# Hybrid encoder layer: one split copy of x without its norm, mean squares taken by token, rope tables built first, queries rotated by halves on VectorE

## The chip, the cores and the metric

The kernel runs on one core of a Trainium2 chip. The metric is the device time of one execution in microseconds (us). Before the change, three runs gave 942.72, 944.30 and 948.27 us, median 944.3 us.

## The reference, cut to what matters

One layer of an encoder over 512 tokens with 1024 features, in float32:

```python
h = rmsnorm(x, g_mix)                      # x * rsqrt(mean(x*x) + EPS) * g_mix
proj = h @ w_in                            # 1024 x 5376
aq, ak, av, hq, hf_f, hf_b, hi, hg, gate_a, gate_b = split(proj)
attn_o = bidir_gqa(aq, ak, av, q_norm, k_norm)     # RMSNorm per head, axial rotary, 8 q heads, 2 kv heads
hgrn_o = hgrn2_bidir(hq, hf_f, hf_b, hi, hg, ...)  # gated recurrence, 4 heads, two directions, chunks of 32
merged = sigmoid(gate_a) * (attn_o @ w_attn_branch) + sigmoid(gate_b) * (hgrn_o @ w_hgrn_branch)
x = x + merged @ w_out
x = x + hier_moe(rmsnorm(x, g_ffn), ...)   # 32 experts, top 2 of one group of 8
```

The norm of a token is one number per row of `h`. So `rmsnorm(x, g) @ w` equals `((x * g) @ w)` with each row multiplied by that number afterwards; the change turns on this. The rotary step takes neighbouring pairs (a, b) of a head to (a cos - b sin, a sin + b cos).

## The kernel before, in words

**Precision.** A float32 product is made of three TensorE passes: each operand is split into a high part and the rest (`h_`, `l_`), and `mm3` (lines 257 to 260) adds high x high, high x low and low x high into the same PSUM bank. Activations are split once, weights when they arrive: `wsplit` (lines 241 to 255) takes a loaded weight tile `wr` of 128x1024, has ScalarE copy it to `wh` (line 250) and VectorE subtract (line 251, `wl`). There are two `wh` and two `wl` buffers, so a split cannot start before TensorE is done with the split two before it.

**Projections.** `w_in` is cut into chunks. Seven "token" chunks of 256 columns (`proj_tok`, 96 matmuls of 128x256 each, two weight tiles of 48 matmuls) put tokens on the partitions: chunk 0 holds keys and values, 1 and 2 the queries, 3 and 4 the values of the recurrence, 5 and 6 its output gates. Twenty-eight "feature" chunks of 128 columns (`proj_fm`, 24 matmuls of 128x512, one weight tile) put features on the partitions: for each of the four recurrence heads two forget gates and a query, then 16 branch gates.

**The start.** SP issues all loads, in the order in which the code is written; there are three `wr` buffers. x arrives transposed in eight pieces `xr` of 128x512. For each, lines 184 and 185 make a first split set `yh`, `yl` of x times `g_mix` without the norm (tile name `m`); ScalarE squares the piece and GpSimd adds the squares up (lines 190 and 191). Chunk 0 runs on this first set, piece by piece as it comes. `norm_x` (lines 204 to 217) sums the squares over partitions with a matmul by ones (line 207), works out the inverse root as a 128x512 tile `rbc`, and transposes it to get `rst`, one number per token (line 216). Chunks 1 and 2 also run on the first set; their norm comes in later through `rst`. Meanwhile `norm_parts` (lines 219 to 228) makes a second split set `xh`, `xl` (tile name `x`) with the norm in it: per piece one VectorE multiply (line 224), one ScalarE copy (225) and one GpSimd subtraction (226). All later projections, but chunk 3, run on the second set.

**Queries and keys.** After chunk 3 the pool of the x pieces is closed, a new pool is opened in its memory, and the rope tables are loaded and multiplied by the q and k norms (lines 332 to 343, tiles `cg` and `sg`). Lines 351 to 375 take the mean squares per head and rotate: ScalarE makes a copy `sw` with the pair elements swapped (368), GpSimd multiplies it by the sine table (372), VectorE multiplies by the cosine table (373), adds (374) and scales by the norms (375), for k in four 128x128 steps and for all eight q heads in four 128x512 steps.

**The heads.** For each recurrence head h: attention scores of two q heads (`att_scores`: scores in PSUM, a maximum over four tiles on VectorE, line 423, then over partitions with GpSimd's `partition_all_reduce`, line 424, a subtraction on VectorE, 426, and an exponential on ScalarE, 427), the recurrence in both directions (`hgrn_dir`), one token chunk, the attention output (`att_out`, lines 435 and 441), and the recurrence's output. GpSimd also does small steps of `hgrn_dir` (lines 524, 540, 545 to 547, 561) and scales the output gates (481). Each forget gate, query and branch gate leaves PSUM by one VectorE `tensor_scalar` with a lower bound (lines 519, 631 and 600).

**The rest.** The branches are multiplied by their gates, `w_out` is applied, the router picks experts, and the weights of all 32 experts stream in (line 781) through a ring of buffers; the first ring buffers become free when the projections are done.

**The order of the work.** SP's queue and the expert matmuls follow the code. On the other queues a list scheduler sorts the instructions by its own cost model; each queue then runs strictly in that order.

## Time and profile before

| | |
|---|---|
| median of 3 runs | 944.3 us |
| the profiled execution | 945.72 us, its span 944.0 us |
| mean granted TensorE clock | 0.988 |
| TensorE busy | 880.5 us (93%) |
| VectorE busy | 439.1 us (47%) |
| ScalarE, GpSimd busy | 267.4 us, 125.8 us |
| read from HBM | 245.11 MB, 264 GB/s over the span |

PE is TensorE's matmuls, PEld its weight loads, DVE VectorE, ACT ScalarE, POOL GpSimd, SP SyncE. In a timeline row the first number is the start, the second the time that the merged instructions cover, both in us; then the engine, the line, the operation, out<-in by tile names, the shape and the count, and in brackets the idle time ahead and what ended it. In a table by windows each engine has its busy us and its count; PEclk is the granted clock. Matmuls overlap, so their own durations (0.39 us for 128x512) are longer than the distance from one start to the next.

### The profile page before, as it was taken

What the parts mean: (1) busy time and instruction counts of PE and PEld (TensorE: products, weight loads), DVE (VectorE), ACT (ScalarE), POOL (GpSimd) and SP (SyncE); (2) the same over time, 40 slices, a digit from 0 to 9 for tenths busy, and PEclk for the clock granted to TensorE, in tenths of its full rate; (3) what the DMA queues carried; (4) which work ended last, traced back from release to release, by engine and by line L of the source; (5) the groups of instructions that cost most, each with busy time, mean ns of one, the idle gap of its engine ahead of it and who ended that gap; (6) DMA issues with size and microseconds to landing.
All of it is one profiled execution on the core that took longest, in us unless ns stands there. A gap on an engine that the chain in (4) does not pass through costs nothing. (4 is left out here: it accounts for less than half of the span.)

```text
span 944.0 us, 12699 instructions
## 1 busy us (share of the span) xinstructions
PE 880.5 (93%) x5098; PEld 556.5 (59%) x5099; DVE 439.1 (47%) x805; ACT 267.4 (28%) x461; POOL 125.8 (13%) x136
## 2 busy tenths in 40 slices
PE   6899989998999999999899999999979889799896
PEld 5798758784867888889744433444424344243433
DVE  6999857876864445433524222423213132031233
ACT  5556646665662545431100000000000000000000
POOL 4543322223310011100111000000000000000000
PEclk9999999998999999999999999999999999999998
DMA  6222201111111222896789999999999999999993
GB/s 225 70 99 90 68 23 68 46 53 60 45 68 62 95 90 89 315 416 249 291 335 348 408 420 417 419 418 420 417 420 420 417 420 419 419 419 419 420 405 133
DMA packets 49646, 246.25 MB, mean 261 GB/s; under 512 B 7024, under 2 KB 12912, under 8 KB 25776
## 3 DMA queue, kind: packets, MB, share of 16 engines
q1 hardware_dynamic: 44304, 238.32, 63.3%
q0 software_dynamic: 2160, 3.94, 1.2%
q10 hardware_dynamic: 3120, 3.15, 1.0%
q8 instruction: 42, 0.69, 0.3%
q14 instruction: 20, 0.16, 0.1%
HBM read 245.11 MB, written 4.19 MB: 264 GB/s over the span
## 5 line engine op out<-in xcount | busy, mean ns | idle before, releaser
L1062 PE MATMUL b<-e,wr 128*64 128x512 f32 x720 | 177.0, 597 | 9.4 <-DMA e<-in_wu 8.7
L1062 PEld LDWEIGHTS b<-e,wr 128*64 128x64 f32 x720 | 56.7, 136 | 104.2 <-issue 82.5
L1069 ACT ACTIVATE gt<-b,sw 128x512 f32<-128x512 f32 x16 | 11.0, 687 | 320.4 <-PE b L1062 320.4
L1090 DVE TENSOR_TENSOR t<-b,t 128x512 fp32r<-128x512 f32 (+1 forms) x33 | 22.2, 673 | 148.5 <-ACT t L1089 148.5
L1087 PE MATMUL b<-e,gt 128*64 128x512 f32 (+1 forms) x368 | 81.7, 575 | 9.6 <-DMA e<-in_wd 8.8
L260 PE MATMUL b<-x,wl 128*128 128x512 f32 x224 | 88.3, 394 | 1.0 <-DVE wl L251 1.0
L258 PE MATMUL b<-x,wh 128*128 128x512 f32 x224 | 88.1, 393 | 0.8 <-ACT hv L330 0.8
L259 PE MATMUL b<-x,wh 128*128 128x512 f32 x224 | 88.0, 393 | 0.0
L250 ACT ACTIVATE wh<-wr 128x1024 fp32r<-128x1024 f32 (+1 forms) x60 | 61.4, 1025 | 80.0 <-PE b L259 47.3
L251 DVE TENSOR_TENSOR wl<-wr,wh 128x1024 fp32r<-128x1024 f32 (+1 forms) x60 | 78.1, 1302 | 11.3 <-ACT wh L250 11.1
L1062 PE MATMUL b<-x,wr 128*64 128x512 f32 x264 | 64.0, 597 | 2.7 <-DMA x<-in_wu 2.7
L1087 PEld LDWEIGHTS b<-e,gt 128*64 128x64 f32 x368 | 26.5, 137 | 60.9 <-issue 45.2
L258 PE MATMUL b<-wh,m 128*128 128x256 f32 x176 | 51.1, 294 | 10.7 <-ACT wh L250 6.5
L1070 DVE SCALAR_TENSOR_TENSOR gt<-b,sw,gt 128x512 f32<-128x512 f32 x16 | 12.0, 750 | 104.1 <-PE b L1062 94.4
L1022 POOL DMA_INDIRECT xs<-xd,ix x15 | 15.3, 1019 | 290.1 <-DVE sw L1025 155.7
L1089 ACT ACTIVATE t<-b 128x512 fp32r<-128x512 f32 (+1 forms) x33 | 19.3, 584 | 122.1 <-PE b L1087 122.1
L259 PE MATMUL b<-wl,m 128*128 128x256 f32 x176 | 51.9, 295 | 1.8 <-DVE wl L251 1.7
L260 PE MATMUL b<-wh,m 128*128 128x256 f32 x176 | 51.1, 292 | 1.3 <-DVE m L185 1.3
L1106 PE MATMUL b<-t,wl 128*128 128x512 f32 (+1 forms) x132 | 51.4, 392 | 0.0
L1107 PE MATMUL b<-t,wl 128*128 128x512 f32 (+1 forms) x132 | 50.5, 385 | 0.4 <-DVE t L1090 0.4
L260 PEld LDWEIGHTS b<-x,wl 128*128 128x128 f32 x224 | 42.1, 188 | 10.7 <-DVE wl L251 1.5
L258 PEld LDWEIGHTS b<-x,wh 128*128 128x128 f32 x224 | 42.1, 188 | 10.2 <-ACT hv L330 1.0
(328 smaller groups left out, 1594.9 us busy)
## 6 DMA issues: line engine op xcount, KB each, us to landing
e<-in_wg SPq DMA_DIRECT2D x45, 1024.0 KB, 19.9
e<-in_wu SPq DMA_DIRECT2D x45, 1024.0 KB, 20.4
e<-in_wd SPq DMA_DIRECT2D x42, 1024.0 KB, 19.9
x<-in_wd SPq DMA_DIRECT2D x19, 1024.0 KB, 19.9
x<-in_wg SPq DMA_DIRECT2D x17, 1024.0 KB, 17.7
x<-in_wu SPq DMA_DIRECT2D x16, 1024.0 KB, 19.9
wr<-in_wfm SPq DMA_DIRECT2D x28, 512.0 KB, 3.5
wr<-in_wtok SPq DMA_DIRECT2D x12, 512.0 KB, 3.4
```

The lines of the kernel that those rows point to most:

```text
L250: SA.activation(h_[:, ks], r[:, ks], AF.Copy)
L251: V.tensor_tensor(l_[:, ks], r[:, ks], f(h_)[:, ks], op=ALU.subtract)
L258: PE.matmul(o, ah, bh, start=first, stop=False)
L259: PE.matmul(o, ah, bl, start=False, stop=False)
L260: PE.matmul(o, al, bh, start=False, stop=last)
L1022: G.indirect_dma_start(xs[q, b], None, xd[:, :], bass.IndirectOffsetOnAxis(ap=ix[:, b], axis=0), bounds_check=S - 1, oob_is_err=False)
L1062: PE.matmul(o[j * 64:(j + 1) * 64, :], hT[half][:, k, b * P + j * 64:b * P + (j + 1) * 64], ring[(n, e, half)](k), start=(half == 0 and k ...
L1087: PE.matmul(o[j * 64:(j + 1) * 64, 0:w], hidT[:, k * P + j * 64:k * P + (j + 1) * 64], ring[("wd", e, n)](k)[:, c:c + w], start=(k == 0), ...
L1089: SA.activation(y[:, 2 * n, c:c + w], o[:, 0:w], AF.Copy)
L1090: V.tensor_tensor(y[:, 2 * n + 1, c:c + w], o[:, 0:w], f(y)[:, 2 * n, c:c + w], op=ALU.subtract)
L1106: PE.matmul(p_[:, 0:w], l, y[:, 2 * n, c:c + w], start=(i == 0), stop=False)
L1107: PE.matmul(p_[:, 0:w], l, y[:, 2 * n + 1, c:c + w], start=False, stop=(i == len(ys) - 1))
```

## The change

- x is split once, without the norm, into tiles `x` (`yh`, `yl`); `norm_parts` and the second set are gone. Every later projection runs on this one set, and the norm is multiplied in when a result leaves PSUM: by token in token chunks (`scale=rst`, or a `tensor_scalar` per token tile), and in feature chunks by `normed`, a `tensor_tensor` with `rbc` from PSUM and then a `tensor_scalar` for the lower bound.
- The mean squares no longer come from the transposed pieces. x is loaded a second time by token, four tiles `xt` of 128x1024 (2 MB), and ScalarE squares each with a running sum. `rst` comes from that directly; `rbc` is built from it by four VectorE broadcasts and four TensorE transposes (`norm_wide`). The matmul by ones and GpSimd's sums are gone.
- The x pieces have four buffers in place of eight; the `at` tiles three in place of four. The loads of w chunk 1, the rope tables, `xt` and the identity stand right behind the x pieces in SP's queue.
- The rope tables have a pool of their own and are built first. `rotate` runs once for k and once for each half of q, behind the chunk that yields it; the swapped product is two VectorE instructions on every second element, and ScalarE's swapped copy and GpSimd's product are gone.

```diff
+    big = [tl(U, [P, 4, 512], "x", F32R, bufs=4) for _ in range(4)]
     for k in range(NK):
-        r = tl(RA, [P, 512], "xr", bufs=8)
+        r = tl(RA, [P, 512], "xr", bufs=4)
         SY.dma_start(r, A["xT"][:, k, :])
...
-        h_, l_ = mt(F32R), mt(F32R)
+        h_, l_ = big[k // 4][:, k % 4], big[2 + k // 4][:, k % 4]
         SA.activation(h_, r, AF.Copy, scale=gmix[:, k:k + 1])
         V.scalar_tensor_tensor(l_, r, gmix[:, k:k + 1], f(h_), op0=ALU.mult, op1=ALU.subtract)
-        if k == 0:
-            SA.activation(sqs, r, AF.Square)
-        else:
-            sq = tl(RA, [P, 512], "sq", bufs=2)
-            SA.activation(sq, r, AF.Square)
-            G.tensor_tensor(sqs, sqs, sq, op=ALU.add)
...
+    w1 = [tl(U, [P, 4, 256], "wr", bufs=3)]
+    SY.dma_start(w1[0], A["wtok"][1, :, 0:4])
+    qkn = cload("qkn", [P, 2, 64], pool=C1)
+    rope = cload("rope", [P, 2, NT, 64], pool=RB)
+    xts = []
+    for t in range(NT):
+        xts.append(tl(RA, [P, D], "xt", bufs=4))
+        SY.dma_start(xts[t], A["xtok"][:, t, :])
+    ident = cload("ident", [P, P])
...
+            SA.activation(tl(RA, [P, D], "sq"), xts[t], AF.Square, accum_out=ms[:, t:t + 1])
...
+            wide = tl(RA, [P, P], "wide", bufs=4)
+            V.tensor_copy(wide, rst[:, t:t + 1].to_broadcast([P, P]))
+            PE.transpose(p_[:, t * P:(t + 1) * P], wide, ident)
...
-            V.scalar_tensor_tensor(xr[k], xr[k], gmix[:, k:k + 1], rbc, op0=ALU.mult, op1=ALU.mult)
-            SA.activation(h_, xr[k], AF.Copy)
-            G.tensor_tensor(l_, xr[k], f(h_), op=ALU.subtract)
...
+    def normed(z, p_):
+
+        V.tensor_tensor(z, p_, rbc, op=ALU.mult)
+        V.tensor_scalar(z, z, -ZMAX, None, op0=ALU.max)
...
-            SA.activation(sw.rearrange("p (c b) -> p c b", b=2), src.rearrange("p (c b) -> p c b", b=2)[:, :, ::-1], AF.Copy)
...
-            G.tensor_tensor(t2.rearrange("p (h d) -> p h d", d=64), sw.rearrange("p (h d) -> p h d", d=64), sb, op=ALU.mult)
+            for i in range(2):
+                V.tensor_tensor(t2.rearrange("p (h c b) -> p h c b", c=32, b=2)[:, :, :, i],
+                                o.rearrange("p (h c b) -> p h c b", c=32, b=2)[:, :, :, 1 - i],
+                                sg[:, w, t, :].rearrange("p (c b) -> p c b", b=2)[:, :, i].unsqueeze(1)
+                                .to_broadcast([P, nh, 32]), op=ALU.mult)
             V.tensor_tensor(ov, ov, cb, op=ALU.mult)
             V.tensor_tensor(o, o, t2, op=ALU.add)
             V.tensor_tensor(ov, ov, b3(qn[:, t, a:b], nh, 64), op=ALU.mult)
...
-            V.tensor_scalar(o, res[j], -ZMAX, None, op0=ALU.max)
+            for t in range(2):
+                V.tensor_scalar(o[:, t], res[j][:, t], rst[:, 2 * j + t:2 * j + t + 1], -ZMAX, op0=ALU.mult, op1=ALU.max)
...
-        V.tensor_scalar(z, p_, -ZMAX, None, op0=ALU.max)
+        normed(z, p_)
```

The scheduler's order moves too. First VectorE's queue where the weights of chunks 1 and 2 are split. Before, from the fifth of the eight products by `rbc` (L224, `xr` are the pieces of x) to the second half of chunk 2 (`wl_445` and `wl_449` are its halves):

```order
L224 SCALAR_TENSOR_TENSOR xr_122<-xr_122,c_gmix_80,rbc_291 128x512
L224 SCALAR_TENSOR_TENSOR xr_133<-xr_133,c_gmix_80,rbc_291 128x512
L224 SCALAR_TENSOR_TENSOR xr_142<-xr_142,c_gmix_80,rbc_291 128x512
L224 SCALAR_TENSOR_TENSOR xr_152<-xr_152,c_gmix_80,rbc_291 128x512
L251 TENSOR_TENSOR wl_445<-wr_440,wh_444 128x1024
L216 COPY rst_304<-hg_299 128x4
L347 TENSOR_TENSOR rs_99_712<-rst_304 128x4
L251 TENSOR_TENSOR wl_449<-wr_442,wh_448 128x1024
```

And after, between the first and the second half of chunk 1, at whose second half (`wl_364`) it ends (`t_60` holds squares of k, `t_61` and `t_62` swapped products of k, `c_lb` the lower bounds):

```order
L212 TENSOR_SCALAR ms_280<-ms_280 128x4
L343 TENSOR_REDUCE qs_321<-t_60_324 128x4x2
L358 TENSOR_TENSOR qk_314<-qk_314,cg_270 128x128
L315 TENSOR_TENSOR lmx_301<-c_lb_260 128x8
L358 TENSOR_TENSOR qk_314<-qk_314,cg_270 128x128
L359 TENSOR_TENSOR qk_314<-qk_314,t_61_335 128x128
L317 TENSOR_TENSOR c_lb_260<-c_lb_260,lmx_301 128x8 x2
L203 TENSOR_TENSOR rst_49_291<-rst_290 128x4
L359 TENSOR_TENSOR qk_314<-qk_314,t_62_341 128x128
L248 TENSOR_TENSOR wl_364<-wr_256,wh_363 128x1024
```

The products by `rbc` that stood ahead of a weight split are gone. Ahead of `wl_364` now stand steps of the rotation of k, among them a row that needs all four sums of squares (L212) and one that needs a constant loaded late (L315).

Second, GpSimd's queue in the second recurrence head. A row that reads only ISA stands wherever the queue goes from ordinary instructions to the all-reduce or back; the ISA row with tile names is the all-reduce itself. Before (`at_1389` and `at_1542` are the maxima of q heads 2 and 3):

```order
L547 TENSOR_TENSOR log_134_836<-log_134_836 128x4x2
L561 TENSOR_TENSOR qt_1628<-e_277_1575,fac_1617 128x512
L424 ISA
L424 ISA at_1389<-at_1388 128x512
L424 ISA at_1542<-at_1541 128x512
L524 ISA
L524 TENSOR_TENSOR k_1967<-k_1967,sg_1969 128x512
```

And after (`at_1369` and `at_1524` are the same two maxima):

```order
L549 TENSOR_TENSOR log_117_811<-log_117_811 128x4x2
L425 ISA
L425 ISA at_1369<-at_1368 128x512
L563 ISA
L563 TENSOR_TENSOR qt_1611<-e_260_1557,fac_1600 128x512
L425 ISA
L425 ISA at_1524<-at_1523 128x512
L526 ISA
L526 TENSOR_TENSOR k_1953<-k_1953,sg_1955 128x512
```

The two all-reduces stood side by side; now the product `qt` stands between them, with an ISA row on each side.

Third, the same queue in the third recurrence head. Before (`at_1899` is the maximum of q head 4):

```order
L540 COPY end_137_839<-z_2081 128x4x4
L545 TENSOR_TENSOR log_133_835<-log_133_835 128x4x4
L546 TENSOR_TENSOR log_133_835<-log_133_835 128x4x2
L547 TENSOR_TENSOR log_133_835<-log_133_835 128x4x2
L424 ISA
L424 ISA at_1899<-at_1898 128x512
L561 ISA
L561 TENSOR_TENSOR qt_2138<-e_361_2085,fac_2127 128x512
```

And after (`at_1884` is the same maximum):

```order
L542 COPY end_120_814<-z_2068 128x4x4
L425 ISA
L425 ISA at_1884<-at_1883 128x512
L547 ISA
L547 TENSOR_TENSOR log_116_810<-log_116_810 128x4x4
L548 TENSOR_TENSOR log_116_810<-log_116_810 128x4x2
L549 TENSOR_TENSOR log_116_810<-log_116_810 128x4x2
L563 TENSOR_TENSOR qt_2126<-e_344_2072,fac_2115 128x512
```

Here the number of ISA rows is the same, but the three small sums of the backward direction now stand behind the all-reduce.

## The prediction

> **What bounds the kernel now.** I read the page first, for the span and the DMA rate by slices, then busy time by windows, then who waited for whom, then timelines around the waits.

> ```profile
> span 944.0 us, 12699 instructions
> ...
> GB/s 225 70 99 90 68 23 68 46 53 60 45 68 62 95 90 89 315 416 249 291 335 348 408 420 417 419 418 420 417 420 420 417 420 419 419 419 419 420 405 133
> ```

> ```profile
> 24.00:66.00 42.00, 37.44 (x298) 36.76 (x296) 38.09 (x64) 21.97 (x43) 22.58 (x15) 0.96 0.27 95
> 138.00:184.00 46.00, 46.00 (x375) 35.30 (x373) 38.03 (x69) 28.68 (x50) 10.56 (x15) 1.00 0.17 58
> 184.00:238.00 54.00, 50.26 (x382) 37.14 (x381) 38.56 (x68) 31.94 (x55) 15.96 (x18) 0.94 0.15 50
> 480.00:944.00 464.00, 430.77 (x2032) 185.20 (x2028) 128.85 (x256) 30.28 (x49) 16.78 (x17) 0.99 0.97 398
> ```

> ```profile
> 388.08 2.02 SPq L781 DMA_DIRECT2D e<-in_wg  x2
> ```

> From 480 us on the DMA engines are 97% busy at 398 GB/s: the expert weights set the pace. Their first load leaves at 388.08 us, when the projections free the buffers, and the router follows on TensorE's results. So the last 560 us are a block that starts when the projections end. The change touches only what is ahead of it, where TensorE is nearly always busy; a microsecond saved there should move the whole block. What TensorE loses ahead of it is few, long waits:

> ```profile
> PE pq L435 <- ACT m L427: 6.9, 2, 3.7
> PE b L258 <- ACT wh L250: 6.5, 1, 6.5
> PE b L258 <- ACT vt L318: 4.2, 1, 4.2
> ```

> ```profile
> 23.54 1.02 PE L207 MATMUL hg<-sqs,ones 128*128 128x512 f32 x2
> ...
> 40.61 0.39 PE L258 MATMUL b<-wh,m 128*128 128x256 f32 x1 [4.18 <-ACT vt L318]
> ...
> 65.24 0.38 PE L383 MATMUL pq<-c_ident,qk 128*128 128x128 f32 x2
> 66.41 0.50 PE L258 MATMUL b<-x,wh 128*128 128x512 f32 x1 [0.79 <-ACT hv L330]
> ...
> 73.64 0.50 PE L260 MATMUL b<-x,wl 128*128 128x512 f32 x1 [1.04 <-DVE wl L251]
> ...
> 84.49 0.39 PE L260 MATMUL b<-x,wl 128*128 128x512 f32 x1
> 84.71 0.28 PE L258 MATMUL b<-wh,x 128*128 128x256 f32 x1
> 84.83 0.28 PE L259 MATMUL b<-wl,x 128*128 128x256 f32 x1
> ...
> 226.79 5.94 PE L435 MATMUL pq<-m,ones 128*64 128x512 f32 x13 [3.74 <-ACT m L427]
> ```

> Starts lie 0.12 us apart for 256 columns and 0.22 for 512, so a token chunk is 96 x 0.12 = 11.5 us and a feature chunk 24 x 0.22 = 5.4. Chunk 0 ends at 23.54. The wait at 40.61 is for the PSUM banks of chunk 0, read only once `rst` is known; VectorE shows why that is late:

> ```profile
> 15.70 3.45 DVE L185 SCALAR_TENSOR_TENSOR m<-xr,c_gmix,m 128x512 fp32r<-128x512 f32 x2
> 20.76 0.75 DVE L185 SCALAR_TENSOR_TENSOR m<-xr,c_gmix,m 128x512 fp32r<-128x512 f32 x1
> 29.12 8.50 DVE L224 SCALAR_TENSOR_TENSOR xr<-xr,c_gmix,rbc 128x512 f32<-128x512 f32 x8
> 39.75 0.15 DVE L216 COPY rst<-hg 128x4 f32<-128x4 f32 x1
> ```

> The same instruction takes 1.73 us while GpSimd adds squares and 0.75 when it does not. The eight products by `rbc` and the weight split behind them push `rst` to 39.75.

> **What the change takes away.** (a) Chunk 0: without GpSimd the two splits of 1.73 fall to 0.75, as do the steps ahead of them; but with four `xr` buffers the last four loads wait for earlier splits. Bounds: a gain of 4.9 us (five slow VectorE steps) and none; I take 3.5, nearer the first, since the loads that wait are two steps ahead. (b) `rst` no longer stands behind L224: the wait of 4.2 goes, and with it the half clock that follows. In 24:66 the granted clock is 0.96, so 42 x 0.04 = 1.7 us are lost; together 5.9. What is late next is VectorE itself, below. (c) The matmul by ones, 0.5. (d) The holes at 66.41 and 73.64, 1.0 and 1.2 beyond the usual distance: both are VectorE or ScalarE behind with the big rotation, which now lies chunks earlier. Sum: 12.1 us.

> **What it adds at the start.** SP now issues 2 MB of `xt` ahead of the second half of chunk 1's weights.

> ```profile
> wr<-in_wtok SPq DMA_DIRECT2D x12, 512.0 KB, 3.4
> ```

> Behind the x pieces stand about 3.5 MB up to those weights. At 390 to 420 GB/s, which the later slices show, that is 8 to 9 us, from some 12 us on; the half tile lands at about 22 to 23, is copied and split through VectorE's row behind the squares, and is ready near 26.2. TensorE wants it at 20 + 5.8 = 25.8. I take 1 us of wait; bounds 0 and 6, the latter at the first slice's 225 GB/s. The four squares on ScalarE lie in time in which it is less than 60% busy.

> VectorE takes on the rotation:

> ```profile
> L251 DVE TENSOR_TENSOR wl<-wr,wh 128x1024 fp32r<-128x1024 f32 x56 | 73.1, 1307 | 10.3 <-ACT wh L250 10.2
> L423 DVE TENSOR_TENSOR at<-sc,at 128x512 f32<-128x512 f32 x16 | 11.0, 685 | 1.7 <-ACT m L421 1.5
> L1034 DVE TENSOR_SCALAR wl<-c_iota,sw 128x512 fp32r<-128x512 f32 x16 | 7.0, 482 | 1.2 <-PE b L1087 1.2
> L355 DVE TENSOR_REDUCE qs<-t 128x16 f32<-128x1024 f32 x2 | 2.4, 1211 | 0.0
> L373 DVE TENSOR_TENSOR qk<-qk,cg 128x128 f32<-128x128 f32 x4 | 1.1, 283 | 0.7 <-ACT sw L368 0.7
> L340 DVE TENSOR_TENSOR cg<-c_rope,c_qkn 128x256 f32<-128x256 f32 x2 | 0.8, 422 | 0.8 <-DMA c_rope<-in_rope 0.8
> L910 DVE TENSOR_REDUCE r_e<-r_em 128x32 f32<-128x128 f32 x1 | 0.4, 376 | 0.0
> ```

> Half of q costs four tiles of two half products of 128 elements and three steps of 256: 4 x (2 x 0.283 + 3 x 0.422) = 7.3 us, the sum of squares 1.2, seven small steps at 0.15 1.1, two weight splits 2.6: 12.2 us, against 11.5 of TensorE. These are durations, and neighbours overlap a little, so VectorE just keeps up; I count 0, with up to 2 us for the two chunks. The half products read and write every second element, which no VectorE product here does. Nearest are the contiguous one (0.283) and a strided reduction of as many elements (0.376); 16 products at 0.093 more are 1.5 us, inside that bound. [...]

> So the lead at the first recurrence head is 12.1 - 1 = 11.1 us.

> **What it changes in the heads.** Twelve gate evictions there become a product from PSUM (0.685, as the old eviction) and a bound from SBUF: 0.482 each, 1.4 us per head on VectorE, which has 83% in 138:184. Most hides behind TensorE; on the chains to the all-reduce I count 0.3 per head, 1.2 in all (bounds 0 and 5.8, all of it). The 16 branch gates come where VectorE is half idle: 0.

> GpSimd's own order matters more.

> ```profile
> 157.82 1.80 POOL L424 PARTITION_ALL_REDUCE at<-at  x1 [5.91 <-DVE wl L251]
> 166.60 1.78 POOL L424 PARTITION_ALL_REDUCE at<-at  x1 [6.97 <-DVE at L423]
> 176.95 1.28 POOL L524 TENSOR_TENSOR k<-k,sg 128x512 f32<-128x512 f32 x1 [8.57 <-ACT sg L522]
> ...
> 203.92 1.80 POOL L424 PARTITION_ALL_REDUCE at<-at  x1 [5.71 <-PE hg L581]
> 212.79 1.05 POOL L561 TENSOR_TENSOR qt<-e,fac 128x512 f32<-128x512 f32 x1 [7.07 <-ACT gt L476]
> 213.81 3.83 POOL L481 TENSOR_TENSOR hg<-hg,c_hnorm 128x256 f32<-128x256 f32 x4
> 223.54 1.80 POOL L424 PARTITION_ALL_REDUCE at<-at  x1 [5.90 <-issue]
> ```

> ```profile
> 148.29 0.62 PE L420 MATMUL sc<-m,m 128*128 128x512 f32 x2
> ...
> 195.62 0.62 PE L420 MATMUL sc<-m,m 128*128 128x512 f32 x2
> ```

> Each passage between ordinary work and an all-reduce takes 5.7 to 7.1 us in which GpSimd does nothing, even where its inputs are there (`issue`). In the second head two all-reduces lay side by side, 8.8 us apart; now `qt` stands between them: passage, 1.1, passage, which puts the second 1.8 + 7.1 + 1.1 + 5.9 = 15.9 behind the first. On the old time axis: the first starts at 156.3 (it no longer stands behind `qt`), the second at 172.2 and ends at 174.0, and the first exponential, a subtraction of 0.7 and 0.6 of ScalarE later, is there at 175.3. TensorE, from the scores at 148.29, now has some 51 matmuls of 256, 51 of 512 and smaller things before it needs it: some 22.5 us, to 171.0. A wait of 4.3, and as the old waits of that length cost the half clock, 1.7 more: +6.0.

> In the third head the small sums move behind the first all-reduce, which for that starts 2.5 us earlier (201.4). `qt` and the gate scaling then end at 216.6 against 217.6, so the second all-reduce is 1 us earlier, while the backward transposes wait about 2 us for the late sums, at a place where no half clock follows. The 3.74 us wait at 226.79 and its clock (0.94 in 184:238, 3.2 us) go; 2.1 + 0.6 come. Sum -4.2. The first head has the same passages as before, the fourth too: 0.

> **The sum**: -11.1 + 1.2 + 6.0 - 4.2 = -8.1 us. The profiled execution took 945.72 us, 1.7 of them around its span, and would take 937.6. It lies 1.4 above the median of 944.3; on that the forecast is 936.2 us.

> **Rivals.** A: VectorE becomes the bound of the start. For: 12.2 against 11.5 per chunk, and every weight split queued behind the rotation. Against: GpSimd no longer slows it. If each of the six half chunks is 1.2 us late, 7 of the 11 go: -1, 943 us.

> B, slower: GpSimd's passages become the bound of the second head. The extra two passages and `qt` are 7.1 + 5.9 + 1.1 = 14.1 us; if GpSimd has no slack there, TensorE waits for all of it and twice the half clock, 14.1 + 3.4 = 17.5 in place of 6.0, and the third head's forward direction, behind yet another passage, gives back nothing of its 4.2: -11.1 + 1.2 + 17.5 = +7.6, 952 us. It decides from a wait of 12 us at that L436. Against: in the old trace GpSimd waits for data for 6.97 of the 8.8 us there. [...]

> C: both head waits vanish, as the scheduler meant them to: -11.1 - 4.2 + 1.2, 930 us. For: the old second head shows none. Against: 15.9 us between the two maxima.

> D: the expert stream hides it all, 944.3 us. Against: its first load waits for TensorE's results.

> **Chances.** Forecast 0.60 (932 to 941), A 0.18, B 0.09, C 0.08, D 0.05. Measurements of this kernel tell about 0.5% (4.7 us) from no change: faster is below 939.6, slower above 949.0. Faster: nine tenths of the forecast, C, and a third of A: 0.68. Slower: B, 0.09. The rest, 0.23. The range leaves out B and takes in C's 930 and the forecast with every bound of the start against it (6 us late weights, 2 of VectorE): 929 to 946.

> **What would show it.** Right: chunk 0 ends near 20 us, the first L384 transposes of k come at 56 in place of 65, no wait of 4 us before it, L436 of the second head waits 3 to 6 us for ScalarE, the third head's wait is under 2 us, and the first expert load leaves near 380. Wrong: rows of TensorE waiting for `wl` in 20 to 60 us (A), a wait over 12 us at L436 (B), none (C), or an early first load with an unchanged end (D).

## The result, and the profile after

The changed kernel takes 955.75 us (median of 6 runs, 954.27 to 958.72) against 944.71 us (6 runs, 942.72 to 948.27) of the kernel before beside it: a ratio of 1.0116, 95% interval 1.0097 to 1.0134. The forecast was 936.2 us. The change makes the kernel slower by 11 us, and the prediction was wrong in sign. The profiled execution has a span of 954.9 us, 10.9 more than before:

```profile
span 954.9 us, 12714 instructions
```

Where the time goes is read from rows that both kernels have. These are TensorE's transposes of the queries (four at once) at the start of each recurrence head, the first expert load, and the last router matmuls. Of the kernel before:

```profile
81.51 0.60 PE L383 MATMUL pq<-c_ident,qk 128*128 128x128 f32 x4
137.03 0.60 PE L383 MATMUL pq<-c_ident,qk 128*128 128x128 f32 x4
184.76 0.60 PE L383 MATMUL pq<-c_ident,qk 128*128 128x128 f32 x4
238.85 0.60 PE L383 MATMUL pq<-c_ident,qk 128*128 128x128 f32 x4
453.58 1.28 PE L816 MATMUL hg<-c_wr,gt 128*128 128x36 f32 x8
```

Of the kernel after (the first expert load was at 388.08 before):

```profile
69.46 0.60 PE L384 MATMUL pq<-c_ident,qk 128*128 128x128 f32 x4
125.27 0.60 PE L384 MATMUL pq<-c_ident,qk 128*128 128x128 f32 x4
181.59 0.60 PE L384 MATMUL pq<-c_ident,qk 128*128 128x128 f32 x4
242.29 0.60 PE L384 MATMUL pq<-c_ident,qk 128*128 128x128 f32 x4
395.33 0.39 SPq L783 DMA_DIRECT2D e<-in_wg  x1
465.41 1.22 PE L818 MATMUL hg<-c_wr,gt 128*128 128x36 f32 x8
```

The differences, after minus before, and what each stage adds. The scheduler's order of TensorE's own queue moves too. Of the 128x512 matmuls of the feature chunks, the trace has 50 ahead of the first head (60 before the change), 131 ahead of the second (137), 197 ahead of the third (205) and 284 ahead of the fourth (274); at the first expert load the counts are about equal (835 and 833). The third column counts a matmul that was put off as 0.22 us still to be done, and one that was done early as 0.22 us in hand. It is an estimate, and the stages are taken from it:

| at | difference, us | with equal work, us | this stage, us | forecast of the stage, us |
|---|---|---|---|---|
| first head | -12.0 | -9.8 | -9.8 | -11.1 |
| second head | -11.8 | -10.5 | -0.7 | +0.3 |
| third head | -3.2 | -1.4 | +9.1 | +6.3 |
| fourth head | +3.4 | +1.2 | +2.6 | -3.9 |
| first expert load | +7.2 | +7.2 | +6.0 | +0.3 |
| last router matmuls | +11.8 | +11.8 | +4.6 | 0 |

So the start gained nearly what was forecast, and everything behind it gave back twice as much. The row "third head" ends the stage of the second head, the row "fourth head" that of the third, and so on. The table by windows shows the same stages. The columns are the busy us and the count of each engine, then the granted clock, the DMA share and GB/s:

```profile
0.00:58.00 58.00, 49.29 (x392) 48.67 (x394) 41.36 (x127) 29.73 (x53) 1.22 (x17) 1.00 0.57 196
138.00:184.00 46.00, 40.55 (x316) 27.65 (x315) 28.89 (x50) 23.39 (x41) 8.61 (x9) 0.96 0.14 47
184.00:238.00 54.00, 46.43 (x366) 35.66 (x365) 37.26 (x69) 26.14 (x46) 12.74 (x16) 0.94 0.13 44
480.00:944.00 464.00, 439.52 (x2078) 189.04 (x2079) 127.86 (x258) 29.90 (x48) 18.11 (x18) 1.00 0.98 401
```

In 138:184 TensorE was busy for all of the 46 us before; now it is for 40.55, and the clock falls to 0.96. The expert stage is as it was, 401 GB/s against 398: a block that moves as a whole.

**The second head.** GpSimd's row, and the matmul that waits for it:

```profile
148.30 1.80 POOL L425 PARTITION_ALL_REDUCE at<-at  x1 [5.92 <-PE hg L583]
156.81 1.39 POOL L563 TENSOR_TENSOR qt<-e,fac 128x512 f32<-128x512 f32 x1 [6.71 <-ACT z L634]
164.34 1.80 POOL L425 PARTITION_ALL_REDUCE at<-at  x1 [6.14 <-issue]
167.58 1.98 PE L436 MATMUL pq<-m,ones 128*64 128x512 f32 x4 [5.28 <-ACT m L428]
```

The second all-reduce starts 16.0 us behind the first, where 15.9 were forecast, and TensorE waits 5.28 us (forecast 4.3).

**The third head.** GpSimd, then ScalarE:

```profile
203.52 1.80 POOL L425 PARTITION_ALL_REDUCE at<-at  x1 [6.09 <-DVE k L557]
212.16 0.21 POOL L547 TENSOR_TENSOR log<-log 128x16 f32<-128x16 f32 x1 [6.83 <-issue]
212.50 0.19 POOL L549 TENSOR_TENSOR log<-log 128x8 f32<-128x8 f32 x1
```

```profile
202.87 0.62 ACT L478 ACTIVATE gt<-gt 128x512 f32<-128x512 f32 x1
212.73 0.26 ACT L550 ACTIVATE fac<-log 128x72 f32<-128x72 f32 x1 [9.23 <-POOL log L549]
214.84 2.18 ACT L428 ACTIVATE m<-m 128x512 f32<-128x512 f32 x4
```

The maximum is there at 205.3, and VectorE subtracts it at once, but the exponentials of line 428 run at 214.84. Ahead of them in ScalarE's queue stands `fac`, which needs the small sums, and these now stand behind the all-reduce and a passage of 6.83 us. ScalarE does nothing for 9.23 us, and a wait of TensorE of 7.51 us follows, the longest in the heads:

```profile
205.36 2.50 DVE L427 TENSOR_TENSOR m<-m,at 128x512 f32<-128x512 f32 x4 [2.41 <-POOL at L425]
215.51 1.97 PE L436 MATMUL pq<-m,ones 128*64 128x512 f32 x2 [7.51 <-ACT m L428]
```

**The router.** ScalarE, VectorE and TensorE around 435 us (ACTq is ScalarE's sequencer):

```profile
433.34 4.67 ACTq L840 DMA_DIRECT2D xd<-hv  x2
438.05 0.42 ACT L810 ACTIVATE junk<-hv 128x256 f32<-128x256 f32 x1 [6.97 <-DMA wr<-in_wo]
438.59 0.16 DVE L844 TENSOR_TENSOR ss<-ss 128x4 f32<-128x4 f32 x1 [6.43 <-ACT junk L810]
438.67 0.42 DVE L815 COPY gt<-hg 128x256 f32<-128x256 f32 x1
439.14 1.06 PE L818 MATMUL hg<-c_wr,gt 128*128 128x36 f32 x4 [3.82 <-DVE gt L815]
```

`xd` are the writes of the middle result to memory, and ScalarE issues them. ScalarE's queue of the kernel after, with the semaphores that each row waits for (those named DMAHW are called lanes here), and of the kernel before at the same two writes:

```
after   L840 DMA xd<-hv_3749 128x256 [waits DMAHW4_49]
        L840 DMA xd<-hv_3749 128x256 [waits DMAHW6_49,DVE_49]
before  L838 DMA xd<-hv_3740 128x256 [waits DMAHW5_49]
        L838 DMA xd<-hv_3740 128x256 [waits DMAHW6_49]
```

In the new order one more weight load and two expert loads stand ahead of the two writes. That the two lanes belong to an expert load issued at 423.81 and a `w_out` load issued at 425.86 is the author's reading; no row names the load that holds a lane. The times agree with it. Both loads are under way while the DMA engines move 418 GB/s, and each write leaves when one of them lands: the expert load takes 9.5 us, to 433.3, and the first write leaves at 433.34; the `w_out` load takes 11.7 us, to 437.6, and the second leaves at 437.68. In the kernel before, the same two writes left at 423.07 and 423.57, and ScalarE waited for no DMA there. In the kernel after it stands still for 6.97 us. Its square stands behind the second write, behind the square VectorE's sum (L844), behind that the copy that the router matmul needs.

### The profile page after: what moved, and what is told of

Read it like the earlier page. It is cut to its first block, busy times and chain, and to the rows that moved or that the text cites. A ratio compares the mean times of both kernels' runs of the same rounds, so it can differ in the third digit from the quotient of the medians.

```text
span 954.9 us, 12714 instructions
## 1 busy us (share of the span) xinstructions
PE 883.1 (92%) x5096; PEld 555.3 (58%) x5097; DVE 432.0 (45%) x868; ACT 261.6 (27%) x448; POOL 88.9 (9%) x113
## 5 line engine op out<-in xcount | busy, mean ns | idle before, releaser
L248 DVE TENSOR_TENSOR wl<-wr,wh 128x1024 fp32r<-128x1024 f32 (+1 forms) x60 | 71.8, 1199 | 17.4 <-ACT wh L247 17.0
L255 PE MATMUL b<-wh,x 128*128 128x256 f32 x192 | 54.9, 289 | 6.6 <-ACT wh L247 6.6
L256 PE MATMUL b<-wl,x 128*128 128x256 f32 x192 | 55.2, 288 | 0.0
L257 PE MATMUL b<-wh,x 128*128 128x256 f32 x192 | 54.8, 286 | 0.0
L255 PEld LDWEIGHTS b<-x,wh 128*128 128x128 f32 x224 | 42.1, 188 | 12.6 <-issue 1.7
L256 PEld LDWEIGHTS b<-x,wh 128*128 128x128 f32 x224 | 42.1, 188 | 9.3 <-issue 0.8
## 6 DMA issues: line engine op xcount, KB each, us to landing
wr<-in_wfm SPq DMA_DIRECT2D x28, 512.0 KB, 3.5
wr<-in_wtok SPq DMA_DIRECT2D x12, 512.0 KB, 3.6
```

The source lines that it names most:

```text
L248: V.tensor_tensor(l_[:, ks], r[:, ks], f(h_)[:, ks], op=ALU.subtract)
L255: PE.matmul(o, ah, bh, start=first, stop=False)
L256: PE.matmul(o, ah, bl, start=False, stop=False)
L257: PE.matmul(o, al, bh, start=False, stop=last)
```

## The experiments

Three theories for the 20 us between forecast and result. **G**: GpSimd's order in the second and third head. **V**: VectorE's extra work in the heads (12 bounds of 0.42 us on top of 12 products), GpSimd only standing by. **L**: the lanes of the writes. Ratios are against the kernel before, run beside each.

**One product to VectorE.**

```diff
-        G.tensor_tensor(c4(qt), c4(e1), b4(way(EY[:, :, 4:8])), op=ALU.mult)
+        (V if h == 1 and fw else G).tensor_tensor(c4(qt), c4(e1), b4(way(EY[:, :, 4:8])), op=ALU.mult)
```

> The changed kernel with one product moved: in the second recurrence head, forward direction, VectorE and not GpSimd makes `qt`. By its queue GpSimd then has the two all-reduces of that head side by side again, and in the third head the small sums and `qt` stand ahead of the all-reduce. Theory G (GpSimd's order in the second and third head makes the loss): the wait of 5.45 us at 162 and its half clock (1.7) go, and of the wait of 7.68 us at 207 and its half clock (3.4) what was not there before (about 3.8): 10 to 12 us, 944 to 946 us. Theory V (VectorE's extra work in the heads makes the loss, GpSimd only waits for it): no change within 1 us, 955 us, or 0.6 slower, since VectorE has one product more.

Measured: 946.38 us, ratio 1.0016 (0.9991 to 1.0041). The second head's all-reduces, the third head's `qt` and all-reduce, and its `fac`:

```profile
154.13 1.80 POOL L425 PARTITION_ALL_REDUCE at<-at  x1 [5.85 <-issue]
164.28 1.78 POOL L425 PARTITION_ALL_REDUCE at<-at  x1 [8.34 <-DVE at L424]
...
195.83 1.59 POOL L563 TENSOR_TENSOR qt<-e,fac 128x512 f32<-128x512 f32 x1 [0.37 <-ACT fac L550]
203.43 1.80 POOL L425 PARTITION_ALL_REDUCE at<-at  x1 [6.01 <-DVE hg L480]
```

```profile
195.49 0.26 ACT L550 ACTIVATE fac<-log 128x72 f32<-128x72 f32 x1 [0.62 <-POOL log L549]
```

The second all-reduce now waits for its data, not for a passage, and `fac` is no longer held up. Moving one instruction changed the scheduler's order in the next head as well, on GpSimd and on the other engines. Some 9.5 us of the 11 are back by the ratios, just short of the 10 to 12 expected: G holds against V, though VectorE has more work than before. What the single product is worth this run can't say; the reverse below can.

**The third head's small sums to VectorE.**

```diff
-        G.tensor_tensor(Y[:, :, 0:4], ...
-        G.tensor_tensor(Y[:, :, 8:11:2], ...
-        G.tensor_tensor(Y[:, :, 11:13], ...
+        (V if h == 2 and fw else G).tensor_tensor(Y[:, :, 0:4], ...
+        (V if h == 2 and fw else G).tensor_tensor(Y[:, :, 8:11:2], ...
+        (V if h == 2 and fw else G).tensor_tensor(Y[:, :, 11:13], ...
```

> The changed kernel with the three small sums of the third head's forward direction on VectorE in place of GpSimd; GpSimd's order in the second head stays. Theory G: ScalarE's `fac` no longer waits for sums that stand behind an all-reduce, so the exponentials queued behind it start on time: the wait of 7.68 us at 207 and its half clock of 3.4 go, but the second maximum's wait of about 4 that the old kernel had there may come back with its clock: 4 to 11 us less, 945 to 952 us. The second head keeps its wait of about 5. Theory V: no change, 955 us.

Measured: 951.02 us, ratio 1.006 (1.0038 to 1.0081).

```profile
198.44 0.26 ACT L550 ACTIVATE fac<-log 128x72 f32<-128x72 f32 x1 [0.50 <-POOL log L549]
```

```profile
168.14 1.97 PE L436 MATMUL pq<-m,ones 128*64 128x512 f32 x4 [5.09 <-ACT m L428]
227.47 1.97 PE L436 MATMUL pq<-m,ones 128*64 128x512 f32 x4 [3.69 <-ACT m L428]
```

`fac` is early again and the wait of 7.51 us is gone, the second head's is as it was, and the third head has its wait of the kernel before back, 3.69 us for 3.74. By the ratios this run gives back 5.3 us, and the first experiment 4.2 more: so the two orders cost 4 to 5 us each, the second head's by subtraction only.

**The writes by GpSimd.**

```diff
-            SA.dma_start(xd[t * P:(t + 1) * P, c * 256:(c + 1) * 256], acc[t][c // 2][:, cs])
+            G.dma_start(xd[t * P:(t + 1) * P, c * 256:(c + 1) * 256], acc[t][c // 2][:, cs])
```

> The changed kernel with the 16 writes of the middle result to memory issued by GpSimd and not by ScalarE. Theory L (two of these writes wait on ScalarE's queue for the semaphore lane of an expert load still in flight, and the last w_out weights are split behind them): the wait of 4.1 us at 434 and the half clock behind it go, 4 to 6 us less, 950 to 952 us. The rival (the expert loads fill the DMA engines, so the weights would be late anyway): no change, 955 us.

Measured: 953.26 us, ratio 1.0078 (1.0049 to 1.0107). The first expert load leaves where it did, at 395.36, and then ScalarE and the router matmuls run on (they were at 438.05 and 439.14):

```profile
395.36 3.00 SPq L783 DMA_DIRECT2D e<-in_wg  x2
...
431.44 0.42 ACT L810 ACTIVATE junk<-hv 128x256 f32<-128x256 f32 x1
...
435.48 0.53 PE L818 MATMUL hg<-c_wr,gt 128*128 128x36 f32 x4
```

In the queues only the 16 writes differ from the kernel after. L holds in place: the router matmul starts 3.7 us earlier behind the same first load. In size it falls short: the ratio drops by 0.0038, 3.6 us, just under the 4 to 6 expected, and the two intervals touch (this one ends at 1.0107, that of the kernel after starts at 1.0097). One word in the expectation was wrong: what stood behind the writes was ScalarE's square and, through VectorE's queue, the copy for the router matmul, not the last weights.

**Without the bound.** In feature chunks the lower bound of the gates is not computed.

```diff
         V.tensor_tensor(z, p_, rbc, op=ALU.mult)
-        V.tensor_scalar(z, z, -ZMAX, None, op0=ALU.max)
```

> The changed kernel with the lower bound of the gates in the feature chunks left out (one VectorE instruction of 0.42 us less for each of 28 chunks; this step of the computation is not done). GpSimd's order in the second and third head becomes the good one as well. Theory V: VectorE is what the heads wait for, so this is at least 5 us faster than the kernel with `qt` on VectorE: 940 us or less. Theory G alone: within 2 us of that kernel, 943 to 946 us.

Measured: 943.47 us, ratio 0.997 (0.9951 to 0.9989). That is 2.9 us less than the first experiment: between the two expectations. But each of these two kernels still has a loss of its own behind the first expert load, so the comparison was made again with the writes on GpSimd, further down.

**The reverse, on the kernel before.** One tiny GpSimd instruction on the first maximum of the second head, first a copy, then a product:

```diff
         G.partition_all_reduce(mr, mx, channels=P, reduce_op=bass.bass_isa.ReduceOp.max)
+        if h == 2:
+            G.tensor_copy(tl(C1, [P, 1], "dm"), mr[:, 0:1])
```

```diff
+            G.tensor_tensor(tl(C1, [P, 1], "dm"), mr[:, 0:1], mr[:, 0:1], op=ALU.mult)
```

> The kernel before, with one GpSimd copy of 128x1 from the first maximum of the second head, which lands between that head's two all-reduces. By its queue a copy stands there without an ISA row on either side. Theory G (the passage between the all-reduce and products costs 6 to 7 us each way, the work between them almost nothing): no change from the kernel before, within 1.5 us. If any ordinary work between the two cost a passage: as the next one, 2 to 8 us slower.

> The same, with a product of 128x1 in place of the copy; by its queue an ISA row then stands on each side of it. Theory G: the second all-reduce starts 7 + 6 us behind the end of the first, near 172.7 in place of 166.6, the passage behind it moves as much; old TensorE had some 4 us of slack there, so 2 to 8 us slower than the kernel before. Theory V (GpSimd's order does nothing by itself): no change.

Measured: with the copy 945.93 us, ratio 1.0 (0.9981 to 1.0019); with the product 950.23 us, ratio 1.0046 (1.0025 to 1.0067). With the copy, and with the product:

```profile
158.19 1.80 POOL L424 PARTITION_ALL_REDUCE at<-at  x1 [6.02 <-DVE wl L251]
160.06 0.70 POOL L426 COPY dm<-at 128x1 f32<-128x1 f32 x1
166.97 1.78 POOL L424 PARTITION_ALL_REDUCE at<-at  x1 [6.20 <-PE hg L662]
```

```profile
156.46 1.80 POOL L424 PARTITION_ALL_REDUCE at<-at  x1 [5.98 <-DVE wl L251]
165.47 0.18 POOL L426 TENSOR_TENSOR dm<-at 128x1 f32<-128x1 f32 x1 [7.21 <-PE hg L662]
171.60 1.80 POOL L424 PARTITION_ALL_REDUCE at<-at  x1 [5.95 <-issue]
```

A product of 0.18 us puts the second all-reduce 13.3 us behind the end of the first (156.46 + 1.80 to 171.60) and costs the kernel about 4.4 us. The order alone does it: in the queues of all five engines, the product and its two ISA rows are the only difference from the kernel before. TensorE's longest wait for it comes one head later, where the old 3.74 us grow to 6.47. What fills the 7.21 us ahead of the product and the 5.95 ahead of the all-reduce no run here shows. The copy follows 0.07 us behind the all-reduce, so it pays nothing on the way out; the way back can't be read, since VectorE had the next maximum ready only at 166.87.

**Both repairs, with and without the bound.** The product on VectorE and the writes on GpSimd; then the kernel without the bound, with the writes on GpSimd.

> The changed kernel with both repairs: `qt` of the second head's forward direction on VectorE, and the writes of the middle result issued by GpSimd. Theories G and L: the gains of the two single repairs add but for what the first kernel already had of the second (its own loss ahead of the router is about 2.5 us): 942 to 944 us, 2 to 4 less than the kernel before. If the expert stream refilled what is gained: no change from the kernel with `qt` on VectorE, 946 us.

> The changed kernel without the lower bound of the gates in feature chunks (this step is not done) and with the writes issued by GpSimd. Against the kernel with both repairs, it differs by VectorE's work alone in the heads. Theory V for the last part of the heads (VectorE without idle time from 243 to 270): 4 to 6 us less than that kernel, 937 to 940 us. If VectorE's extra work is covered: the same within 1.5 us.

Measured: 941.32 us, ratio 0.9955 (0.9934 to 0.9975), and 937.72 us, ratio 0.9911 (0.9884 to 0.9939). The first is just under its 942 to 944, the second inside its 937 to 940. Their first expert loads:

```profile
386.17 5.74 SPq L783 DMA_DIRECT2D e<-in_wg  x4
```

```profile
380.78 6.05 SPq L782 DMA_DIRECT2D e<-in_wg  x4
```

Without the bound the time is 3.6 us less, and the load leaves 5.4 us earlier. Twelve bounds in the heads at 0.42 us are 5.0 us: if the bound alone makes the difference, most of it lies on the path, not the small part that was forecast. In the profile of the kernel after, the row of the bound for the forget gates is

```profile
L283 DVE TENSOR_SCALAR z<-z 128x512 f32<-128x512 f32 x8 | 3.4, 422 | 0.1
```

V holds too, as a smaller part, but its size is not shown. The kernel with the bound also has `qt` once on VectorE (some 0.69 us, which `kt`, a product of the same shape, takes there in the kernel after), and the two differ in GpSimd's order in the first head and in the order of the other engines' queues, so the 3.6 us are not the bound's alone for certain.

**The bound on ScalarE.** The eight forget gates keep their bound, as a relu of z + 43, and the 43 is taken off in the exponential; the writes are on GpSimd.

```diff
-        normed(z, p_)
-        SA.activation(u, z, AF.Exp, scale=-1.0)
+        V.tensor_tensor(z, p_, rbc, op=ALU.mult)
+        SA.activation(z, z, AF.Relu, bias=zmx)
+        SA.activation(u, z, AF.Exp, scale=-1.0, bias=zmx)
```

> The changed kernel with the writes issued by GpSimd, and the lower bound of the eight forget gates on ScalarE, as a relu of z + 43 whose 43 the exponential behind it takes off again; VectorE so has 0.42 us less in each recurrence direction and the bound is kept. GpSimd's order in the second and third head becomes the good one; the first head's small sums move behind its first all-reduce. Theory V: most of what leaving the bound out brought: 938 to 941 us. If ScalarE's 0.69 us more on the gate's chain weigh as much as VectorE's 0.42 less: 941 to 943, as with both repairs alone.

Measured: 938.74 us, ratio 0.9918 (0.9899 to 0.9936). This lies inside the range that V gave. It is the whole computation, and it beats both kernels by the ratios: the kernel before by 0.8%, the kernel after by 2%.

**Two controls on the kernel before.** The writes on GpSimd; and three `at` tiles in place of four.

> The kernel before, with the writes of the middle result issued by GpSimd. Theory L (the wait is a matter of which lane a write gets, and the old kernel's writes got lanes that were free): no change, within 1.5 us of the kernel before. If writes on ScalarE's queue cost time as such: 3 to 5 us faster.

> The kernel before with three `at` tiles in place of four, the one part of the change not yet looked at. Theories G, V and L: no change, within 1.5 us. If the scores wait for a free `at` tile: 2 to 6 us slower.

Measured: 945.1 us, ratio 0.9979 (0.9967 to 0.9992), and 947.11 us, ratio 1.0002 (0.9985 to 1.002). Even where no write waits, GpSimd as their issuer is worth some 2 us by the ratio (0.9 by the medians), so of the 3.6 us of the third experiment a part may be that. The profiled executions tell more of L. From the first expert load to the end, the four changed kernels with the writes on ScalarE take 558.4 to 562.3 us, the four with them on GpSimd 553.0 to 555.0; the kernel before takes 555.9, and 555.6 with its writes on GpSimd. So it is in the changed order that the writes on ScalarE's queue cost time. That the long wait for a lane is all of it is not shown: in the first experiment TensorE waits for the router's copies only 1.0 us, and it too takes 558.4 us. The `at` tiles have no part in the loss.

## Why the prediction was wrong, point by point

**The start: right.** Chunk 0 ends at 20.10 against 23.54, 3.4 us for a forecast of 3.5. The wait of 4.2 us and its half clock (0.52 in 41:44 of the kernel before) are gone (1.00 in the first window), and the waits for the weights of chunk 1 are short:

```profile
20.10 0.28 PE L255 MATMUL sc<-wh,x 128*128 128x256 f32 x1
21.31 0.38 PE L256 MATMUL sc<-wl,x 128*128 128x256 f32 x1 [0.93 <-DVE wl L248]
...
28.59 0.39 PE L256 MATMUL sc<-wl,x 128*128 128x256 f32 x1 [1.15 <-DVE wl L248]
```

The lead at the first head is 12.0 us for a forecast of 11.1, of which 2.2 us are matmuls put off, so 9.8. Rival A falls: from 20 to 60 us no other row of TensorE waits for VectorE. The transposes of k that stood at 65.24 were expected at 56 and are now at

```profile
57.89 0.38 PE L384 MATMUL pq<-c_ident,qk 128*128 128x128 f32 x2
```

**The second head: right in its mechanism, low in size.** Forecast: 15.9 us between the all-reduces, a wait of 4.3 and 1.7 us at half clock, +6.3 for the stage; found 16.0, a wait of 5.28 with a clock of 0.50 behind it (167.5:170.5), and +9.1.

**The third head: the step that failed.** "The 3.74 us wait at 226.79 and its clock (0.94 in 184:238, 3.2 us) go; 2.1 + 0.6 come." The late small sums were followed to their readers on TensorE, the backward transposes, but not to what is queued behind them on ScalarE. There `fac` stands ahead of the exponentials, and these waited for sums they do not use: 7.5 us, in place of 3.74, with the clock as low as it was before (0.94 in 184:238). Forecast -3.9, found +2.6. The second experiment, whose edit moves only the sums, gave back 5.3 us of time by the ratios. Its first load leaves 5.9 us earlier; with equal work, 1.8 us of that come before the fourth head and 4.1 behind it. So the late sums, or the order of the other queues that goes with them, also make most of the stage up to the first load, forecast +0.3, found +6.0; how they reach that far was not taken apart. And where the order was good, the old wait of the third head did not go: besides the 3.69 us above, the kernel with both repairs still has such waits, by who waited for whom (the longest, 3.3, is the third head's):

```profile
PE pq L436 <- ACT m L428: 7.0, 3, 3.3
```

So in these orders that gain was not to be had.

**VectorE in the heads: mis-sized.** "I count 0.3 per head, 1.2 in all (bounds 0 and 5.8, all of it)". The 3.6 to 5.4 us of the runs lie nearer the bound that was not taken, though they are not the bound's alone for certain. VectorE at 83% was read as having room. Weight splits stand in its queue, and the likely reason, an estimate of the author's that no run shows, is that they waited behind the added work as ScalarE's exponentials did behind `fac` (9.23 us).

**The router: left out.** Nothing in the prediction put a cost there; it let the router follow TensorE's results, and the diff has no line there. That the scheduler's order moves also changes which DMA waits for which was seen for SP's queue at the start and not looked for on ScalarE's, 400 us later. 4.6 us.

**The rivals.** B gave 952, close, but by a wait of 12 us or more in the second head, and that was 5.28: it took the right engine, and the wrong head for the rest of its price. D falls: a load that leaves earlier ends earlier (5.3 us later and 4.4 us more time with the product in between, 7.3 earlier and 8 less without the bound), except for what the writes add behind it. C falls with the waits of 5.28 and 7.51 us. At the first load the kernel with both repairs is 1.9 us ahead of the kernel before, the one with the bound on ScalarE 3.7, the one without the bound 7.3, of the 9.8 us of the start; where the rest goes in the heads was not taken apart.

## What to carry to other kernels

When an instruction is moved or made late, follow its queue on every engine that reads it, not only its readers: here ScalarE stood still for 9.23 us at `fac`, and exponentials with other data stood behind it. When a scheduler sets the order, compare the order far from the edit too, for passages on GpSimd (5.95 and 7.21 us around one product of 0.18) and for DMAs issued from a compute engine (6.97 us of ScalarE). A busy share of 83% (138:184 of the kernel before) did not show that VectorE had room: the run that left 5.0 us of bounds out of the heads was 3.6 us shorter, though not by the bound alone for certain. Take the whole added work as the upper price, and keep it in the range. And before stages of two kernels are compared, count whether the same work lies in them.

## What the runs showed of the hardware that was not expected

```profile
L354 DVE TENSOR_TENSOR t<-qk,sg 128x128 f32<-128x128 f32 x16 | 3.6, 284 | 0.4 <-ACT qk L366 0.4
```

They take 0.284 us against 0.283 for the contiguous product of the kernel before.
